# Feed-forward products over both parts of the activations at once, with the two halves of PSUM joined in later turns

## The chip, the cores and the metric

The kernel runs on one core of one Trainium2 chip. The metric is the device time of one execution in microseconds (us); the time before is 1494.89 us, the median of three runs (1494.23 to 1496.46). The engines are PE (TensorE: matrix products, written to PSUM), PEld (its weight loads), DVE (VectorE), ACT (ScalarE) and POOL (GpSimd). SP issues the DMAs.

## The reference

Three transformer blocks over 256 tokens of width 1024, in fp32, batch 1. The first has sliding-window and differential attention, cross attention and a feed-forward part with a squared ReLU. The second and the third are wrapped in SwiGLU feed-forward parts and modulated by a vector c, with a convolution and latent-attention mixer in the one and a sparse attention in the other:

```python
u = rms_norm(x, g_mlp[l]) @ w_up[l]                 # 1024 -> 4096
x = x + jnp.square(jax.nn.relu(u)) @ w_down[l]      # 4096 -> 1024
...
mod = c_act @ ada_w[l] + ada_b[l]                   # 1024 -> 9 x 1024, per layer l
h = modulate(x, norm_g[l, 0], sh1, sc1)
x = x + 0.5 * g1[:, None] * swiglu(h, ff_w13[l, 0], ff_w2[l, 0])   # 1024 -> 2 x 2816 -> 1024
...
def swiglu(h, w13, w2):
    a, b = jnp.split(h @ w13, 2, axis=-1)
    return (jax.nn.silu(a) * b) @ w2
```

SwiGLU runs four times (layer 0 and 1, before and after the mixer). The weights are some 300 MB, each read once.

## The kernel before

**Layout.** Activations lie transposed: channels on the 128 partitions, the 256 tokens (S) along the free axis. A weight tile of 128 x 128 is the stationary side of a product, a chunk of activations of 128 channels the moving one.

**Two parts.** For accuracy every operand is split into a high part (rounded to the fast fp32r format) and a low part (the rest). A product of weights w and activations x is three on PE, high by high, high by low and low by high: `mm3` (L358), 256 columns each. ACT makes the high part of the weights (`whi`), DVE the low one (`wlo`, L415), 1024 columns at a time, which is a group of eight tiles. `hhi` and `hlo` are the parts of a stage's input, `gh` and `gl` those of a feed-forward part's inner activations.

**The stream.** All weights come by DMA through four raw buffers of 1 MB (`raw`, RAW_BUFS = 4), each two groups; `issue` (L386) sends a DMA when a buffer is free, which for weights is after the second group's `wlo`. `pump` (L402) splits three groups ahead of PE; the `wlo` of a group is issued one group behind its `whi`. `run` (L435) takes the steps in a list one after another; each engine works off its own instructions in the order in which they were issued. Work put into `deferred` is issued by `flush` (L430) at the next group.

**The ten feed-forward stages.** `pairs` (L462) runs w_up (16 pairs) and the four w13 (22 pairs each): a pair is two output blocks of 128 channels, 16 tiles, two groups. The first pairs after a norm (the head: three in w13_00, two in each other w13, none in w_up) run on the input before normalisation and keep a form of their own. At the end of a pair an evacuation takes the two blocks out of one PSUM bank: `evac_up` (L1353, ReLU with the norm's factor on DVE, square on ACT) or `evac` in `ff` (L1403, SiLU on ACT, product on DVE, both from PSUM). The split into `gh` and `gl` waits in `deferred`. `singles` (L516) runs w_down (8 output blocks of 32 tiles) and the four w2 (8 blocks of 22); its evacuation `residual` (L1265) adds a block to x and begins the next norm.

**The modulation.** 72 further buffers of 1 MB (`ada`) pass through the same four raw buffers, between the weights, from 97 us on to the first third of w2_10. A piece is scaled in place by ACT and added by POOL (`adacc`, L737); the buffer is free after POOL's last addition. Its sums pass PE into a PSUM bank with the tag "T".

**Pools.** Activations that live long lie in 64 buffers of 256 columns (`g`, GP = 64). PSUM has eight banks: two each with the tags mm, T, S and O.

Of the kernel before, what the change touches and what calls it, by code (L numbers as in the profile page):

```python
# [24 lines left out]
P = 128  # L25
S = 256
# [15 lines left out]
GP = 64  # L42
# [250 lines left out]
class Kernel:  # L293
    def __init__(self, tc, ctx, dram, out):
# [63 lines left out]
    def mm3(self, out, w, x, start, stop, swap=False):  # L358

        (wh, wl), (xh, xl) = w, x  # L360
        prod = [(wh, xh), (wh, xl), (wl, xh)]
        if swap:
            prod = [(xh, wh), (xh, wl), (xl, wh)]
        for n, (l, r) in enumerate(prod):
            self.mm(out, l, r, start=start and n == 0, stop=stop and n == 2)

# [95 lines left out]
    def pairs(self, name, x, kc, evac, unit0=0, npairs=None, st=None, head=0, tags=("mm", "mm"),  # L462
              biased=None):
# [25 lines left out]
        for s0 in range(0, total, sub_tiles):  # L489
            def fn(hi, lo, s0=s0):  # L490
                for t in range(s0, min(s0 + sub_tiles, total)):
# [1345 lines left out]
```

## Time and profile before

| | us |
|---|---|
| median of the runs | 1494.89 |
| the profiled execution | 1491.65 |
| its span, first to last instruction | 1489.9 |
| PE, DVE, ACT, POOL busy in the span | 1437.3, 1059.5, 918.9, 633.6 |
| w_up, w_down (us from the span's start) | 243 to 340, 343 to 441 |
| w13_00, w2_00 | 441 to 577, 577 to 642 |
| w13_01, w2_01 | 756 to 886, 887 to 954 |
| w13_10, w2_10 | 954 to 1085, 1085 to 1150 |
| w13_11, w2_11 | 1288 to 1416, 1417 to 1480 |

The two digits of a w13 or w2 are the layer and the first or second feed-forward part in it. The ten windows make 980 us, two thirds of the span. The granted PE clock is 1.00 of full speed in every one of them (0.995 over the span). A share of busy time is an average over its window; the chain of waits is followed back from the end of the window, at each step to what released it.

### The profile page before, as it was taken

How to read it: one execution, taken by the hardware profiler on the slowest of the kernel's cores; microseconds unless marked ns; L12 is line 12 of the kernel's file. 1: busy time of each engine (PE TensorE's matmuls, PEld its weight loads, DVE VectorE, ACT ScalarE, POOL GpSimd, SP SyncE). 2: the span in 40 equal slices, each digit the busy share in tenths (PEclk: the TensorE clock that was granted, in tenths of full speed). 3: DMA queues.
4: the chain of work that ended last, by engine and by line, in shares of the span. 5: the costliest groups of instructions: out<-in, count | busy, mean ns of one | idle time of the engine just before them, and what ended most of it. 6: DMA issues, size and time to landing. Idle time of an engine off the chain costs nothing.

```text
span 1489.9 us, 28338 instructions
## 1 busy us (share of the span) xinstructions
PE 1437.3 (96%) x11478; PEld 1374.9 (92%) x11478; DVE 1059.5 (71%) x1643; ACT 918.9 (62%) x1666; POOL 633.6 (43%) x466
## 2 busy tenths in 40 slices
PE   8998999999999999998899999999999999999997
PEld 8886989999989989998799999999999887999997
DVE  7877767776658777689887776677765788765553
ACT  6546767777657567664667666676654665644442
POOL 3002433545874566753356658546453200500021
PEclk9999999999999999999999999999999999999998
DMA  8344646777665777754447877568773620355451
GB/s 319 116 142 170 218 151 227 244 270 273 260 246 199 278 267 272 257 186 170 169 171 272 295 262 296 206 238 300 259 278 132 219 80 25 118 198 196 173 182 45
DMA packets 46067, 312.00 MB, mean 209 GB/s; under 512 B 5232, under 2 KB 7024, under 8 KB 9072
## 3 DMA queue, kind: packets, MB, share of 16 engines
q1 hardware_dynamic: 45936, 310.19, 57.8%
q8 instruction: 90, 1.47, 0.4%
q14 instruction: 41, 0.34, 0.1%
HBM read 309.12 MB, written 1.05 MB: 208 GB/s over the span
## 4 chain that ended last, share of the span: by engine, by line
PE 64%; DVE 16%; ACT 8%; DMA 7%; issue 2%; POOL 1%; SPq 0%; POOLq 0%; ACTq 0%; DVEq 0%
PE mm L356 57%; DVE wlo L415 6%; DMA raw<-w 4%; ACT whi L329 2%; ACT raw L329 2%; PE sc L356 2%; PE o L356 1%; DVE p L849 1%; POOL adacc L737 1%; PE mmt L356 1%; DVE hlo L664 1%; DMA raw<-w_up 1%; DMA raw<-w_down 1%; DVE gl L353 1%; ACT p L329 1%
## 5 line engine op out<-in xcount | busy, mean ns | idle before, releaser
L415 DVE TENSOR_TENSOR wlo<-raw,whi 128x1024 fp32r<-128x1024 f32 (+2 forms) x438 | 627.2, 1438 | 52.2 <-ACT whi L329 51.7
L737 POOL TENSOR_TENSOR adacc<-adacc,raw 128x512 f32<-128x512 f32 x252 | 430.8, 1734 | 415.8 <-ACT raw L329 331.4
L356 PE MATMUL mm<-hlo,whi 128*128 128x256 f32 x1960 | 556.6, 284 | 6.0 <-DVE hlo L664 4.1
L356 PE MATMUL mm<-hhi,whi 128*128 128x256 f32 (+1 forms) x1960 | 558.0, 285 | 1.5 <-ACT whi L329 1.5
L356 PE MATMUL mm<-hhi,wlo 128*128 128x256 f32 (+1 forms) x1960 | 553.3, 282 | 5.2 <-DVE wlo L415 5.2
L329 ACT ACTIVATE whi<-raw 128x1024 fp32r<-128x1024 f32 (+2 forms) x438 | 453.2, 1044 | 110.6 <-DMA raw<-w 72.5
L356 PEld LDWEIGHTS mm<-hlo,whi 128*128 128x128 f32 x1960 | 369.9, 189 | 9.6 <-DVE hlo L664 5.6
L356 PEld LDWEIGHTS mm<-hhi,wlo 128*128 128x128 f32 x1960 | 371.2, 189 | 7.3 <-DVE wlo L415 7.0
L356 PEld LDWEIGHTS mm<-hhi,whi 128*128 128x128 f32 x1960 | 370.2, 189 | 5.4 <-DVE wlo L415 1.7
L356 PE MATMUL mm<-gh,whi 128*128 128x256 f32 x960 | 272.6, 284 | 0.0
L356 PE MATMUL mm<-gh,wlo 128*128 128x256 f32 x960 | 271.6, 283 | 0.0
L356 PE MATMUL mm<-gl,whi 128*128 128x256 f32 x960 | 271.6, 283 | 0.0
L356 PEld LDWEIGHTS mm<-gh,whi 128*128 128x128 f32 x960 | 184.2, 192 | 4.3 <-issue 3.4
L356 PEld LDWEIGHTS mm<-gl,whi 128*128 128x128 f32 x960 | 184.2, 192 | 0.0
L356 PEld LDWEIGHTS mm<-gh,wlo 128*128 128x128 f32 x960 | 184.2, 192 | 0.0
L329 ACT ACTIVATE raw<-raw,sc 128x512 f32<-128x512 f32 x252 | 167.0, 712 | 0.6 <-DMA raw<-ada 0.5
L1410 DVE TENSOR_TENSOR ft<-mm,ft 128x256 f32<-128x256 f32 x79 | 33.4, 423 | 110.0 <-ACT ft L329 109.8
L353 DVE TENSOR_TENSOR gl<-ft,gh 128x256 fp32r<-128x256 f32 x120 | 74.0, 628 | 46.2 <-ACT gh L329 46.0
L580 POOL TENSOR_SCALAR xg<-x,M 128x256 f32<-128x256 f32 x40 | 55.9, 1398 | 97.4 <-DVE x L1273 91.2
L329 ACT ACTIVATE p<-sc,nm 128x128 f32<-128x128 f32 (+1 forms) x120 | 49.8, 420 | 66.5 <-DVE r L840 18.7
L329 ACT ACTIVATE ft<-mm 128x256 f32<-128x256 f32 x79 | 29.9, 379 | 96.3 <-PE mm L356 96.1
L596 POOL TENSOR_TENSOR acc<-acc,sq 128x256 f32<-128x256 f32 x60 | 60.8, 1016 | 43.5 <-ACT sq L329 37.0
(298 smaller groups left out, 1878.6 us busy)
## 6 DMA issues: line engine op xcount, KB each, us to landing
raw<-w SPq DMA_DIRECT2D x132, 1024.0 KB, 4.9
raw<-ada SPq DMA_DIRECT2D x72, 1024.0 KB, 6.4
raw<-w_up SPq DMA_DIRECT2D x16, 1024.0 KB, 5.0
raw<-w_down SPq DMA_DIRECT2D x16, 1024.0 KB, 5.2
raw<-hy_in SPq DMA_DIRECT2D x8, 1024.0 KB, 5.2
raw<-w_in SPq DMA_DIRECT2D x6, 1024.0 KB, 7.8
raw<-nsa_in SPq DMA_DIRECT2D x6, 1024.0 KB, 5.0
raw<-w_ck SPq DMA_DIRECT2D x4, 1024.0 KB, 4.9
```

Of the source, the lines that this page charges most:

```text
L329: return self.nc.scalar.activation(out, in_, func, **k)
L353: self.nc.vector.tensor_tensor(lo, src, hi.bitcast(F), OP.subtract)
L356: self.nc.tensor.matmul(out, lhsT, rhs, start=start, stop=stop, skip_group_check=True)
L415: self.behind = lambda hi=hi[:, :b - a], lo=lo[:, :b - a], src=src: self.nc.vector.tensor_tensor(lo, src, hi.bitcast(F), OP.subtract)
L580: nc.gpsimd.tensor_scalar(st["xg", c], xc, gain(c), None, op0=OP.mult)
L596: nc.gpsimd.tensor_tensor(acc, st["acc" + key], sq, OP.add)
L664: nc.vector.scalar_tensor_tensor(*last, op0=OP.add, op1=OP.subtract)
L737: nc.gpsimd.tensor_tensor(half, half, src, OP.add)
L849: nc.vector.tensor_scalar(p[n], p[n], r[:, n:n + 1], None, op0=OP.mult)
L1410: nc.vector.tensor_mul(s, ps[:, 1, :], s)
```

## The change

In the ten stages the three products of a tile become two: `mm2` multiplies the weights' high part with both parts of the activations, which lie side by side, in one product of 512 columns over a whole PSUM bank, and adds the low part by the high activations to one half of that bank. Each block of a wide pair has a bank of its own, so two halves must be summed. `summed` copies one half of each block out with ACT and adds the other with DVE, at the end of the pair; what was the evacuation (`up`) is issued at the next group, and the split into parts one group later. In `singles` each half is added to x in an operation of its own. All other products keep the three of 256 columns (`mm3w`, `mm3`). The activations' buffers become 32 of 512 columns, which hold both parts of one tensor or two tensors of 256 columns; the sums of the modulation move from the PSUM tag T to O.

```diff
-GP = 64
+GP = 32
+PAIRED = {"un", "posi", "mem", "kz", "ra", "tab", "qr", "qd", "kd", "vd", "ck", "cv", "cq", "xpT", "od", "q", "k", "v",
+          "kb", "xg", "vcz", "p0", "cu"}
...
     def g(self, name, dt=F, shape=None):
-        return self.gp.tile(shape or [P, S], dt, name=name, tag="g")
+
+        key = (name if name in PAIRED else "", dt)
+        t = self.half.pop(key, None)
+        n = 1
+        if t is None:
+            n = 0
+            t = self.half[key] = self.gp.tile([P, 2, S], dt, name=name, tag="g")
+        ap = t[:, n, :]
...
+    def two(self, name):
+
+        if name == "gg":
+            self.half.clear()
+        t = self.gp.tile([P, 2, S], R, name=name, tag="g")
+        return t[:, 0, :], t[:, 1, :], t.rearrange("p a b -> p (a b)")
...
+    def summed(self, pss):
+
+        ts = [self.t("ft") for _ in pss]
+        for t, ps in zip(ts, pss):
+            self.act(t, ps[:, 0, :])
+        for t, ps in zip(ts, pss):
+            self.nc.vector.tensor_add(t, ps[:, 1, :], t)
+        return ts
...
+    def mm2(self, out, w, x, start, stop):
+
+        (wh, wl), (xh, _, both) = w, x[:3]
+        self.mm(out.rearrange("p a b -> p (a b)"), wh, both, start=start, stop=False)
+        self.mm(out[:, self.hi_at(x), :], wl, xh, start=False, stop=stop)
...
     def flush(self):
-        for f in self.deferred:
+
+        now, self.deferred = self.deferred, []
+        for f in now:
             f()
-        self.deferred.clear()
...
-                        if r == 0:
+                        if r == 0 and wide:
+                            state["ps"] = [self.ps("mm", [P, 2, S], "mm"), self.ps("mm", [P, 2, S], "T")]
+                        elif r == 0:
                             state["ps"] = self.ps("mm", [P, 2, S], tags[pr % 2])
-                        self.mm3(state["ps"][:, m, :], w, (xh, xl), start=r == 0, stop=k == kc - 1)
+                        if wide:
+                            self.mm2(state["ps"][m], w, x(k), start=k == 0, stop=k == kc - 1)
+                        else:
+                            self.mm3w(state["ps"][:, m, :], w, (xh, xl), start=r == 0, stop=k == kc - 1)
...
-                            state[m] = self.ps("mm", [P, S], "S" if early else "mm")
+                            state[m] = self.ps("mm", [P, S], "S") if early else self.ps("mm", [P, 2, S], "mm")
...
+                    if early:
+                        self.mm3w(state[m], w, x(k)[:2], start=first, stop=k == kc - 1)
+                    else:
+                        self.mm2(state[m], w, x(k), start=first, stop=k == kc - 1)
...
+    def h_part(self, c):
+
+        return self.h[:, c, S:2 * S], self.h[:, c, :S], self.h[:, c, :2 * S], None
...
-                ps = self.ps("ada", [P, 512], "T")
+                ps = self.ps("ada", [P, 512], "O")
...
-                if gate is None:
-                    nc.vector.tensor_add(xc, ps, xc)
-                else:
-                    nc.vector.scalar_tensor_tensor(xc, ps, gate(m), xc, op0=OP.mult, op1=OP.add)
+                for part in (ps,) if len(ps.shape) == 2 else (ps[:, 0, :], ps[:, 1, :]):
+                    if gate is None:
+                        nc.vector.tensor_add(xc, part, xc)
+                    else:
+                        nc.vector.scalar_tensor_tensor(xc, part, gate(m), xc, op0=OP.mult, op1=OP.add)
...
-            for m in range(2):
-                t = self.t("ft")
-                nc.vector.scalar_tensor_tensor(t, ps[:, m, :], 0.0, stu["rbs"], op0=OP.max, op1=OP.mult)
-                self.act(t, t, AF.Square)
-                gh, gl = self.g("gh", R), self.g("gl", R)
-                self.deferred.append(lambda gh=gh, gl=gl, t=t: self.split(gh, gl, t))
-                gg[2 * pr + m] = (gh, gl)
...
+            for m, t in enumerate(self.summed(ps)):
+                g = gg[2 * pr + m] = self.two("gg")
+
+                def up(g=g, t=t):
+                    nc.vector.scalar_tensor_tensor(t, t, 0.0, stu["rbs"], op0=OP.max, op1=OP.mult)
+                    self.act(t, t, AF.Square)
+                    self.deferred.append(lambda: self.split(g[0], g[1], t))
+                self.deferred.append(up)
...
-            else:
-                self.act(s, ps[:, 0, :], AF.Silu)
-                nc.vector.tensor_mul(s, ps[:, 1, :], s)
-            gh, gl = self.g("gh", R), self.g("gl", R)
-            self.deferred.append(lambda: self.split(gh, gl, s))
-            gg[pr] = (gh, gl)
+                self.deferred.append(lambda: self.split(g[0], g[1], s))
+                return
+            s, t = self.summed(ps)
+
+            def up():
+                self.act(s, s, AF.Silu)
+                nc.vector.tensor_mul(s, t, s)
+                self.deferred.append(lambda: self.split(g[0], g[1], s))
+            self.deferred.append(up)
```

PE in w13_11. Before, two tiles, the last of one group of weights (`whi_17261`) and the first of the next; one bank `mm_17368` takes both blocks of the pair:

```order
L356 MATMUL mm_17368<-hhi_15679,whi_17261 128x256
L356 MATMUL mm_17368<-hlo_15680,whi_17261 128x256
L356 MATMUL mm_17368<-hhi_15679,wlo_17262 128x256
L356 MATMUL mm_17368<-hhi_15679,whi_17294 128x256
L356 MATMUL mm_17368<-hlo_15680,whi_17294 128x256
L356 MATMUL mm_17368<-hhi_15679,wlo_17295 128x256
```

After, two tiles of one group, one for each block of the pair; each block has a bank, and `h` holds both parts:

```order
L386 MATMUL mm_15346<-h_13877,whi_15254 128x512
L386 MATMUL mm_15346<-h_13877,wlo_15255 128x256
L386 MATMUL mm_15347<-h_13877,whi_15254 128x512
L386 MATMUL mm_15347<-h_13877,wlo_15255 128x256
L386 MATMUL mm_15346<-h_13877,whi_15254 128x512
```

The product with `whi` has both parts in it, the one with `wlo` follows; the instructions of a tile go from three to two.

ACT in w13_11, one pair of groups. Before, `ft<-mm` is the SiLU out of PSUM:

```order
L329 ACTIVATE whi_16337<-raw_16097 128x1024
L329 ACTIVATE ft_16365<-mm_16312 128x256
L329 ACTIVATE whi_16370<-raw_16097 128x1024
L329 ACTIVATE gh_16368<-ft_16365 128x256
L329 ACTIVATE whi_16403<-raw_16176 128x1024
L329 ACTIVATE ft_16431<-mm_16378 128x256
```

After, two copies out of two banks stand where the SiLU stood; the SiLU is `ft<-ft`:

```order
L350 ACTIVATE gg_14781<-ft_14782 128x256
L350 ACTIVATE ft_14837<-mm_14796 128x256
L350 ACTIVATE ft_14838<-mm_14797 128x256
L350 ACTIVATE whi_14843<-raw_14627 128x1024
L350 ACTIVATE ft_14837<-ft_14837 128x256
L350 ACTIVATE whi_14869<-raw_14682 128x1024
L350 ACTIVATE gg_14836<-ft_14837 128x256
```

The split's high part (`gh`, now `gg<-ft`) has moved from behind the second `whi` of a buffer to behind the first `whi` of the next one, just ahead of the next pair's copies.

DVE in w13 stages, one pair of groups; `raw_16003` and `raw_14462` are buffers of weights. Before:

```order
L1410 TENSOR_TENSOR ft_16299<-mm_16246,ft_16299 128x256
L415 TENSOR_TENSOR wlo_16272<-raw_16003,whi_16271 128x1024
L353 TENSOR_TENSOR gl_16303<-ft_16299,gh_16302 128x256
L415 TENSOR_TENSOR wlo_16305<-raw_16003,whi_16304 128x1024
L1410 TENSOR_TENSOR ft_16365<-mm_16312,ft_16365 128x256
L415 TENSOR_TENSOR wlo_16338<-raw_16097,whi_16337 128x1024
```

After:

```order
L383 TENSOR_TENSOR gg_14616<-ft_14617,gg_14616 128x256
L378 TENSOR_TENSOR ft_14672<-mm_14631,ft_14672 128x256
L378 TENSOR_TENSOR ft_14673<-mm_14632,ft_14673 128x256
L457 TENSOR_TENSOR wlo_14650<-raw_14462,whi_14649 128x1024
L1471 TENSOR_TENSOR ft_14672<-ft_14673,ft_14672 128x256
L457 TENSOR_TENSOR wlo_14679<-raw_14462,whi_14678 128x1024
L383 TENSOR_TENSOR gg_14671<-ft_14672,gg_14671 128x256
L378 TENSOR_TENSOR ft_14727<-mm_14686,ft_14727 128x256
```

Ahead of the first `wlo` of a buffer stand two additions from PSUM, where the SiLU's product stood; the product now stands ahead of the second `wlo`, which frees the buffer, and `gg` behind it, where `gl` stood ahead of it.

## Rows read from the trace of the kernel before

**Rows 1.** The page: busy us (share of the span) xinstructions of an engine.

```profile
PE 1437.3 (96%) x11478; PEld 1374.9 (92%) x11478; DVE 1059.5 (71%) x1643; ACT 918.9 (62%) x1666; POOL 633.6 (43%) x466
```

**Rows 2.** Chain of waits by line: w_up, w_down, w13_00, w2_00, w13_01, w2_01, w13_11.

```profile
by line: PE mm L356 29.3%; DMA raw<-w_up 16.7%; ACT whi L329 12.7%; DVE wlo L415 8.4%; ACT raw L329 7.9%; ACT ft L329 5.4%; DVE gl L353 5.3%; issue 3.5%; ACT gh L329 3.2%; POOL adacc L737 2.7%; PE ada L356 2.0%; DVE ft L1356 1.6%; PE ssum L
by line: PE mm L356 59.3%; DMA raw<-w_down 15.4%; DVE wlo L415 7.4%; POOL adacc L737 4.6%; issue 4.4%; ACT raw L329 2.7%; PE ada L356 1.5%; ACT whi L329 1.2%; DVE hlo L574 0.9%; PE adat L760 0.9%; ACT sq L329 0.8%; DVE x L1271 0.5%; DVE hhi
by line: DMA raw<-w 22.9%; PE mm L356 22.0%; DVE wlo L415 13.0%; ACT whi L329 8.4%; POOL adacc L737 6.0%; ACT raw L329 5.2%; DVE gl L353 3.7%; PE mmt L356 3.2%; ACT ft L329 2.5%; issue 2.4%; DVE hlo L664 1.7%; DVE ft L1407 1.3%; PE ssum L35
by line: PE mm L356 98.1%; PE ada L356 1.6%; PE adat L760 0.6%
by line: PE mm L356 88.3%; DVE hlo L664 2.3%; PE mmt L356 2.2%; DVE wlo L415 2.2%; PE ada L356 0.8%; DVE gl L353 0.7%; DVE hlo L666 0.7%; PE ssum L356 0.6%; DVE ft L1407 0.6%; ACT ft L329 0.4%; PE rb L356 0.4%; PE adat L760 0.3%; DVE un L48
by line: DMA raw<-w 31.8%; PE mm L356 24.1%; DVE wlo L415 12.3%; issue 5.4%; POOL adacc L737 5.2%; ACT whi L329 4.8%; ACT raw L329 4.0%; ACT L334 1.9%; ACT adacc L329 1.8%; ACT hhi L329 1.6%; PE ada L356 1.6%; ACT sq L329 1.5%; DVE x L1273 
by line: PE mm L356 89.1%; DVE hlo L664 2.4%; PE mmt L356 2.2%; DVE wlo L415 2.2%; DVE gl L353 0.7%; DVE hlo L666 0.7%; PE ssum L356 0.6%; DVE ft L1407 0.6%; ACT ft L329 0.4%; PE rb L356 0.4%; DVE un L480 0.3%; ACT rbs L329 0.3%; issue 0.1%
```

**Rows 3.** Windows in w_up, w13_00, w13_01, w13_11: busy us (xcount) of PE, PEld, DVE, ACT, POOL.

```profile
262.00:340.00 78.00, 75.88 (x633) 75.35 (x632) 57.01 (x76) 59.68 (x108) 40.59 (x27) 1.00 0.76 266
460.00:545.00 85.00, 83.20 (x686) 81.97 (x685) 69.09 (x78) 57.85 (x94) 47.71 (x27) 1.00 0.69 250
780.00:850.00 70.00, 70.00 (x589) 70.00 (x588) 51.20 (x51) 49.86 (x78) 45.95 (x26) 1.00 0.80 286
1310.00:1410.00 100.00, 100.00 (x839) 100.00 (x839) 54.49 (x72) 46.25 (x72) 0.00 (x0) 1.00 0.55 191
```

**Rows 4.** Timeline of PE, products of 512 columns: start us, duration us, engine, operation.

```profile
67.74 0.39 PE L356 MATMUL mm<-wlo,hhi 128*128 128x512 f32 x1
...
70.07 0.39 PE L356 MATMUL mm<-whi,hlo 128*128 128x512 f32 x1
...
113.33 0.40 PE L356 MATMUL mm<-wlo,hmh 128*128 128x512 f32 x1
...
115.61 0.39 PE L356 MATMUL mm<-whi,hml 128*128 128x512 f32 x1
```

**Rows 5.** Groups by line: busy us, mean ns of one, then idle time before.

```profile
L1410 DVE TENSOR_TENSOR ft<-mm,ft 128x256 f32<-128x256 f32 x79 | 33.4, 423 | 110.0 <-ACT ft L329 109.8
L329 ACT ACTIVATE ft<-mm 128x256 f32<-128x256 f32 x79 | 29.9, 379 | 96.3 <-PE mm L356 96.1
L353 DVE TENSOR_TENSOR gl<-ft,gh 128x256 fp32r<-128x256 f32 x120 | 74.0, 628 | 46.2 <-ACT gh L329 46.0
L1273 DVE SCALAR_TENSOR_TENSOR x<-mm,M,x 128x256 f32<-128x256 f32 x48 | 23.1, 481 | 67.5 <-PE mm L356 67.4
```

**Rows 6.** Timeline of DVE in w13_01, then of POOL in the same stretch.

```profile
802.53 2.31 DVE L415 TENSOR_TENSOR wlo<-raw,whi 128x1024 fp32r<-128x1024 f32 x1
805.36 0.42 DVE L1410 TENSOR_TENSOR ft<-mm,ft 128x256 f32<-128x256 f32 x1 [0.51 <-ACT ft L329]
...
808.43 1.21 DVE L415 TENSOR_TENSOR wlo<-raw,whi 128x1024 fp32r<-128x1024 f32 x1
...
802.29 5.93 POOL L737 TENSOR_TENSOR adacc<-adacc,raw 128x512 f32<-128x512 f32 x3
```

**Rows 7.** Waits of ACT in w_up, w13_00, w13_01 (two rows), w13_11: us, times, longest.

```profile
ACT ft L329 <- DVE ft L1356: 11.0, 7, 1.9
ACT whi L329 <- DMA raw<-w_up: 7.3, 4, 3.3
...
ACT whi L329 <- DMA raw<-w: 22.2, 7, 5.3
...
ACT whi L329 <- DMA raw<-w: 10.0, 6, 3.2
ACT ft L329 <- PE mm L356: 8.0, 9, 1.8
...
ACT ft L329 <- PE mm L356: 51.5, 17, 3.2
```

More of the change, by code (lines that the diff above doesn't have):

```diff
@@ L303, in __init__ @@
         self.flip, self.now = 0, None
+        self.half = {}
         self.deferred, self.behind = [], None
     def g(self, name, dt=F, shape=None):
-        return self.gp.tile(shape or [P, S], dt, name=name, tag="g")
+        key = (name if name in PAIRED else "", dt)
[5 more added lines that the diff above has]
+        ap = t[:, n, :]
+        if shape:
+            names = " ".join(f"d{i}" for i in range(len(shape) - 1))
+            ap = ap.rearrange(f"p ({names}) -> p {names}", **{f"d{i}": x for i, x in enumerate(shape[1:])})
+        return ap
+    def two(self, name):
[3 more added lines that the diff above has]
+        return t[:, 0, :], t[:, 1, :], t.rearrange("p a b -> p (a b)")
     def w(self, name, shape, dt=F, tag=None, bufs=2):
@@ L356, in mm, with mm3, mm3w, hi_at @@
         self.nc.tensor.matmul(out, lhsT, rhs, start=start, stop=stop, skip_group_check=True)
-    def mm3(self, out, w, x, start, stop, swap=False):
+    def mm3(self, out, w, x, start, stop):
         (wh, wl), (xh, xl) = w, x
[L361 to L364, printed above, removed]
+        for n, (l, r) in enumerate([(xh, wh), (xh, wl), (xl, wh)]):
             self.mm(out, l, r, start=start and n == 0, stop=stop and n == 2)
+    def mm3w(self, out, w, x, start, stop):
+        (wh, wl), (xh, xl) = w, x
+        for n, (l, r) in enumerate([(wh, xh), (wh, xl), (wl, xh)]):
+            self.mm(out, l, r, start=start and n == 0, stop=stop and n == 2)
+    def mm2(self, out, w, x, start, stop):
+        (wh, wl), (xh, _, both) = w, x[:3]
+        self.mm(out.rearrange("p a b -> p (a b)"), wh, both, start=start, stop=False)
+        self.mm(out[:, self.hi_at(x), :], wl, xh, start=False, stop=stop)
+    def hi_at(self, x):
+        return 1 if len(x) > 3 else 0
     def stream_init(self, steps):
@@ L462, in pairs @@
     def pairs(self, name, x, kc, evac, unit0=0, npairs=None, st=None, head=0, tags=("mm", "mm"),
-              biased=None):
+              biased=None, wide=False):
         steps, state = [], {}
@@ L899, in split_out @@
     def split_out(self, ps, name, scale=None):
-        hi, lo = self.g(name + "h", R), self.g(name + "l", R)
+        pair = self.two(name)
+        hi, lo = pair[:2]
         if scale is None:
@@ L905, in split_out @@
             self.nc.vector.scalar_tensor_tensor(lo, ps, scale, hi.bitcast(F), op0=OP.mult, op1=OP.subtract)
-        return hi, lo
+        return pair
     def zeroed(self, name, keep):
@@ L965, in late_loads @@
         nc.sync.dma_start(self.posi[1], self.dram["pos"][:, 1, :])
-        self.mem = [self.g(f"mem{c}") for c in range(KD)]
+        self.mem = [self.g("mem") for c in range(KD)]
         for c in range(KD):
@@ L1067, in mdst @@
         def mdst(c):
-            hm[c] = (self.g(f"hmh{c}", R), self.g(f"hml{c}", R))
+            hm[c] = self.two("hm")
             return hm[c]
@@ L1460, in evac_z @@
                         nc.vector.tensor_mul(a, src, a)
-                        hi, lo = self.g("yh", R), self.g("yl", R)
-                        self.split(hi, lo, a)
-                        y[c] = (hi, lo)
+                        y[c] = self.two("y")
+                        self.split(y[c][0], y[c][1], a)
         scale = 96 ** -0.5
@@ L1474, in qdst @@
         def qdst(c):
[L1475 removed]
+            cqn[c] = self.two("cqn")
             return cqn[c]
         def kdst(c):
[L1479 removed]
+            ckvn[c] = self.two("ckvn")
             return ckvn[c]
```

58 lines of the change are left out of this document (27 added, 31 removed).

## The prediction

> **What bounds the kernel now.** I read the page's engine totals first, then the chain of waits cut by stage, then busy times in steady stretches, then what ScalarE (ACT) waits for. The reader is to see a kernel that TensorE (PE) seems to fill, and in part doesn't. PE is busy 1437.3 of 1489.9 us [rows 1]. But the chain that sets the end lies on PE's products only in some of the ten feed-forward stages [rows 2]: 98.1% of w2_00, 88.3% of w13_01, 89.1% of w13_11 and, with rows like these, w13_10, w2_10 and w2_11. In w_up it is 29.3%, in w13_00 22.0%, in w2_01 24.1%, in w_down 59.3%; there it goes round a loop: a raw weight buffer lands, ACT makes its high part, VectorE (DVE) its low part, the buffer is free, the next DMA goes out. The steady stretches say the same [rows 3]: in w13_11 (no modulation weights, POOL idle) DVE is busy 54% and ACT 46% of the time, in w13_01 73% and 71%, in w_up 73% and 77%, in w13_00 81% and 68%. And ACT has nothing left in w_up: 59.68 us busy and 11.0 + 7.3 us of waits for DVE and DMA make up the 78 us [rows 3, 7], so it never waits for PE there. In w13_00 it waits 22.2 us for DMA, in w13_01 10.0 for DMA and 8.0 for PE, in w13_11 51.5 for PE alone [rows 7].
>
> **The change part by part.** First the products. A tile (128 x 128 weights) takes three products of 256 columns now, and one of 512 and one of 256 after: the same 768 columns, one instruction and one weight load fewer. In w13_11 PE starts 839 products in 100 us [rows 3], one per 119.2 ns. Products of 512 columns run already where weights are the moving side: ten follow each other in 2.33 us and ten in 2.28 us [rows 4], 233 and 228 ns. Two of 256 take 238.4, so a tile saves 5.4 to 10.4 ns; I take the middle, 7.9 ns. The tiles: 16 pairs of w_up and 19 + 3 x 20 pairs of w13 beyond the heads, 16 tiles each, make 256 + 304 + 960; w_down has 256 and each w2 176; 2480 in all. In the six stages whose chain is PE (1488 tiles) the saving is 11.8 us. In the other four I count the chain's share on PE: 256 x 0.293 + 256 x 0.593 + 304 x 0.22 + 176 x 0.241 = 336 tiles, 2.7 us. Sum: 14.5 us saved, of a possible 2480 x 7.9 = 19.6.
>
> The Trainium skill ("TensorE: Matmul & The Clock Gate", section "Back-to-back issue gap") gives a spacing of N/2.4 + 2.5 ns, by which two of 256 columns and one of 512 differ by 2.5 ns only. By that the saving on these 1824 tiles would be an estimated 4.6 us; the rows show 119.2 ns where the page has 109.2, so here each product carries more than the page says, and the rows decide.
>
> Second, joining the halves. Each wide pair gets two ACT copies out of PSUM (379 ns each) and two DVE additions with one side in PSUM (423 ns as the product `ft<-mm,ft`) [rows 5]. The ReLU or the SiLU and its product then work from SBUF. Per pair that is 0.76 us of ACT and 0.85 us of DVE more, beside PE's 48 products (5.72 us before, 5.6 after). In w13_01 DVE's 51.20 us over 12.2 pairs [rows 3] are 4.19 per pair, ACT's 49.86 are 4.08. The product that now reads two SBUF tiles is priced by `gl<-ft,gh`, 628 ns [rows 5], 0.2 more. After: DVE 5.24, ACT 4.84 of 5.6. Both still fit, so I hide them behind PE in w13_01 and w13_10, and more easily in w13_11; if this cover goes, the stage takes DVE's time.
>
> Why could it go? DVE and POOL exclude each other on some operations: from 802.29 us on POOL runs three `adacc` for 5.93 us; a `wlo` that starts beside them takes 2.31 us, one that starts behind them 1.21, and an `ft` product out of PSUM in their midst keeps its 0.42 [rows 6]. The Trainium skill ("SBUF — State Buffer", section "Who interferes with whom") says that a DVE instruction with two SBUF inputs contends with POOL's reads and that one with a single SBUF input does not. This trace agrees (2.31 against 1.21, and 0.42 unmoved). By it the additions are free of POOL and the moved product is not; without it DVE would need 5.04 per pair in w13_01.
>
> In w_up and w13_00 the additions lie on the buffer loop: on DVE they stand ahead of the `wlo` that frees the buffer. In exchange `gl` moves behind that `wlo`, and the product moves between the two `wlo`. Per pair on the loop: 0.85 + 0.63 - 0.42 - 0.63 = 0.43 us. The chain is off PE for 0.71 x 16 + 0.78 x 19 = 26 pairs, so up to 11.2 us; nothing is the other end, since ACT waits for DMA there anyway, and below nothing it could gain the 11.0 us that ACT waits for DVE's `ft` in w_up [rows 7]. I take 5 us: a buffer's freeing is on the chain about every second pair (there are four).
>
> Third, the edge of a stage. Each output block of w_down and w2 is now added to x in two operations; the last one of a stage has the next norm behind it. One more of 481 ns [rows 5], five times: 2.4 us. The other 35 blocks lie beside products.
>
> At nothing: the activations laid side by side (same bytes, same writers); the buffers handed out in pairs (the same 64 halves; the cover is that the long-lived ones sit together, and if a half keeps its partner, one DVE or ACT write waits for a product, some 0.3 us at a time); the modulation rows in the "O" banks (in these stages only the norm's sum uses them); the later split of the activations (the next stage reads the last of them in its third step). PE waits for whole banks, two per row of a pair, which are free after copies and additions, 1.6 us into a pair of 5.6.
>
> Sum: -14.5 + 5 + 2.4 = -7.1 us. The profiled execution, 1491.65 us, is 3.2 under the runs' median of 1494.89; the sum is taken from the former (1484.6) and shifted by that: 1487.8, so 1488.
>
> **The rivals.** R1, PE decides everywhere: faster join work and shorter products let the early stages catch up too. For it: PE is busy 75.88 of 78 us even in w_up [rows 3]. Against it: rows 2. Time: all 2480 tiles, 19.6 - 2.4 = 17.2 less, 1478; with 10.4 ns per tile, 1471.
>
> R2, slower: ACT and DVE become the bound of the two early stages. In w_up ACT's two copies fit in no wait for PE, because there is none: 16 x 0.76 = 12.2 us. In w13_00 the 0.43 us on the loop is paid by each of 19 pairs: 8.2. With 11.8 saved in the PE stages and 2.4 at the edges: +11, 1506. It decides from the point where ACT's busy time and its waits in w_up pass 5.7 us a pair; they stand there now. Against it: waits for DMA shrink when ACT comes later, and ACT's waits for DVE's `ft` may move.
>
> R3, nothing: a product of 512 columns among others of 256 costs what two cost, for instance because the weight load behind it is no longer hidden. For it: the 512s of rows 4 stand among themselves only. Against it: both lie under 238.4. Time: 2.4 us of edges and no gain, 1497, within the bound. The page's rule on spacing named above would lie close to it, with those 4.6 us as a gain.
>
> **How the numbers follow.** Forecast 40% (own range 1481 to 1494), R1 20%, R2 23%, R3 17%. A measurement of this kernel can tell about 0.2%, 3 us, from no change. Faster by more: 0.35 of the forecast's 0.40, all of R1, 0.03 of R3: 0.58. Within: 0.05 of the forecast, 0.10 of R3, 0.01 of R2: 0.16. Slower: 0.26. The range reaches into R1 with half its mass and to R2's value: 1473 to 1506.
>
> **What would show it.** Right: starts of a 512 and the 256 behind it together about 351 ns where three took 358; w13_11 and w2_11 shorter by 2.5 and 1.4 us; w13_01 and w13_10 still on PE in the chain, with DVE above 90% busy; w_up and w13_00 not shorter. Wrong: a `mm` on PE that waits for `wlo` throughout w13_01 (then DVE bounds it and R2 spreads), ACT waiting for PE in w_up (R1), or a 512 at 238 ns or more (R3). A PE that waits for a PSUM bank, or a long wait outside the feed-forward stages, would break what I put at nothing.

## The result: 1.6% slower

The kernel with 512-column products takes 1519.49 us (median of 4 runs, 1515.93 to 1521.71), the kernel before 1495.2 (4 runs, 1494.23 to 1496.46): ratio 1.016, 95% interval 1.0138 to 1.0181. The forecast was 1488, faster. The profiled execution spans 1519.9 us, 30.0 more than the one of before; it is the slowest of its four, while the one of before (1491.65 us) lies below all four of its runs, so the profiles differ by more than the medians' 24.3 us. The page's engine totals, which answer to [rows 1]:

```profile
PE 1439.6 (95%) x8998; PEld 1249.8 (82%) x8998; DVE 1172.8 (77%) x1873; ACT 974.4 (64%) x1856; POOL 627.5 (41%) x466
```

PE is as busy as before with 2480 products fewer; DVE has 113 us more, ACT 55. Which stage pays is read from the starts of each stage's first product (us to the next stage's first product; the last one to the end of the span). The four right-hand columns are kernels of the experiments below. Every column is one execution: where a stage's code is that of before, eight profiles put w_up at 98.7 to 100.5 us, w13_00 at 135.4 to 138.1 and w13_10 at 130.2 to 131.1.

| stage | before | after | sums in PSUM | before, no additions | after, no additions | late stages wide |
|---|---|---|---|---|---|---|
| w_up | 100.2 | 111.9 | 103.8 | 95.7 | 93.9 | 100.3 |
| w_down | 97.4 | 97.3 | 98.3 | 94.3 | 92.6 | 97.4 |
| w13_00 | 136.6 | 140.4 | 136.8 | 131.4 | 129.4 | 135.6 |
| w2_00 | 65.1 | 65.5 | 64.1 | 65.1 | 62.8 | 65.3 |
| hybrid attention | 113.6 | 119.7 | 117.2 | 107.4 | 105.6 | 114.2 |
| w13_01 | 130.5 | 136.2 | 129.7 | 130.5 | 128.4 | 130.2 |
| w2_01 | 67.7 | 69.6 | 70.7 | 65.0 | 62.8 | 67.4 |
| w13_10 | 130.6 | 134.7 | 133.9 | 130.6 | 128.4 | 130.3 |
| w2_10 | 65.5 | 66.1 | 64.2 | 65.1 | 63.6 | 64.0 |
| second attention | 137.2 | 136.9 | 137.2 | 139.0 | 137.6 | 136.7 |
| w13_11 | 128.9 | 126.8 | 126.8 | 129.0 | 126.8 | 126.8 |
| w2_11 and end | 73.4 | 71.7 | 72.2 | 73.3 | 71.8 | 71.3 |

The loss (30.0 us) is w_up 11.7, hybrid attention 6.1, w13_01 5.7, w13_10 4.1, w13_00 3.8 and w2_01 1.9, against 3.9 gained in w13_11 and w2_11, where POOL has nothing to add.

The chain of waits cut by stage, as in [rows 2]: w_up, w13_00, w13_01, w13_11 of the kernel after. It is one chain, followed back from the last instruction of the run, and a window shows the part of it that lies there.

```profile
by line: DVE ft L1413 16.6%; DVE wlo L457 15.7%; ACT whi L350 11.4%; DVE gg L383 11.4%; PE mm L386 10.8%; DVE ft L378 8.1%; ACT raw L350 7.7%; ACT ft L350 7.6%; ACT gg L350 4.1%; ACT adacc L350 2.3%; issue 1.6%; PE ada L386 0.9%; PE ssum L3
by line: DMA raw<-w 24.7%; ACT whi L350 11.1%; DVE wlo L457 9.7%; PE mm L386 9.5%; ACT ft L350 6.6%; ACT raw L350 6.3%; issue 5.7%; POOL adacc L790 5.2%; PE mmt L386 3.1%; DVE ft L1471 2.9%; DVE gg L383 2.6%; ACT adacc L350 2.4%; ACT gg L35
by line: DMA raw<-w 23.9%; PE mm L386 20.8%; ACT whi L350 11.3%; ACT raw L350 8.4%; DVE wlo L457 7.1%; ACT ft L350 6.1%; issue 4.8%; DVE ft L1471 2.7%; ACT gg L350 2.3%; DVE h L715 2.2%; PE mmt L386 2.1%; POOL adacc L790 2.1%; DVE gg L383 1
by line: PE mm L386 89.1%; DVE h L715 2.4%; PE mmt L386 2.3%; DVE wlo L457 2.2%; DVE h L717 0.7%; DVE gg L383 0.7%; PE ssum L386 0.6%; DVE ft L1464 0.6%; ACT ft L350 0.4%; PE rb L386 0.4%; DVE un L523 0.3%; ACT rbs L350 0.3%; issue 0.1%; DV
```

w13_01, 88.3% on PE in [rows 2], is now at 20.8%, and goes round the buffer loop like w13_00. In w_up the largest item is one that was 1.6%: `ft L1413`, the ReLU product that the change moved from PSUM to SBUF. The steady stretches, as in [rows 3] (w_up, w13_00, w13_01, w13_11):

```profile
262.00:350.00 88.00, 78.81 (x419) 65.11 (x418) 70.76 (x97) 65.44 (x131) 40.21 (x26) 0.98 0.64 233
470.00:560.00 90.00, 84.42 (x472) 71.32 (x471) 79.48 (x102) 64.89 (x120) 45.70 (x27) 1.00 0.66 243
800.00:875.00 75.00, 72.37 (x402) 61.41 (x402) 62.99 (x76) 56.94 (x105) 40.82 (x24) 1.00 0.69 255
1340.00:1440.00 100.00, 100.00 (x571) 87.58 (x570) 69.38 (x115) 59.96 (x111) 0.00 (x0) 1.00 0.56 199
```

PE no longer fills w_up (78.81 of 88 us) or w13_01 (72.37 of 75, full before), yet DVE is only 80% and 84% busy: no single engine is full. In w13_11 PE is full, and POOL stands at 0. The products themselves cost what was expected, as two of them in w13_11 show (timeline of PE: start, duration):

```profile
1360.51 0.40 PE L386 MATMUL mm<-h,whi 128*128 128x512 f32 x1
1360.74 0.29 PE L386 MATMUL mm<-h,wlo 128*128 128x256 f32 x1
1360.87 0.40 PE L386 MATMUL mm<-h,whi 128*128 128x512 f32 x1
```

A 512 starts, the 256 follows after 0.23 us and the next 512 0.13 behind that, 0.36 here; over the whole of w13_11 the medians are 232 and 118 ns, and 351 from one 512 to the next, from the starts in the trace.

The groups that answer to [rows 5] (busy, mean ns of one, idle time before), over the whole run:

```profile
L378 DVE TENSOR_TENSOR ft<-mm,ft 128x256 f32<-128x256 f32 x190 | 71.6, 416 | 42.8 <-ACT ft L350 42.8
L383 DVE TENSOR_TENSOR gg<-ft,gg 128x256 fp32r<-128x256 f32 x120 | 68.1, 579 | 45.9 <-ACT gg L350 45.7
L1471 DVE TENSOR_TENSOR ft<-ft 128x256 f32<-128x256 f32 x79 | 65.6, 830 | 14.5 <-ACT ft L350 14.5
L1413 DVE SCALAR_TENSOR_TENSOR ft<-ft,rbs 128x256 f32<-128x256 f32 x32 | 25.1, 825 | 0.0
```

The same view of w13_01 and then of w13_11, DVE:

```profile
L1471 DVE TENSOR_TENSOR ft<-ft 128x256 f32<-128x256 f32 x12 | 9.4, 784 | 4.7 <-ACT ft L350 4.7
...
L1471 DVE TENSOR_TENSOR ft<-ft 128x256 f32<-128x256 f32 x18 | 7.5, 418 | 0.0
```

The added sums, with one side in PSUM, take 416 ns. The moved products, which now read two SBUF tiles (`ft<-ft` names the same pool twice), take 830 and 825; I had priced them at 628. In w13_01 it is 784, in w13_11, without POOL, 418. These means mix two prices. Of the 32 products of w_up the shortest, the median and the longest (ns) are:

```profile
L1413 DVE SCALAR_TENSOR_TENSOR ft<-ft,rbs x32: 410/418/1516, 253.0 to 359.4; 128x256 f32<-128x256 f32 x32
```

In the trace, the 12 that overlap an `adacc` of POOL take 1507 ns on average, the 20 with POOL idle 416 at the median. What holds them up is seen in w_up, in the timelines of DVE and of POOL over one stretch, as in [rows 6]:

```profile
264.09 0.74 DVE L378 TENSOR_TENSOR ft<-mm,ft 128x256 f32<-128x256 f32 x2
264.75 1.21 DVE L457 TENSOR_TENSOR wlo<-raw,whi 128x1024 fp32r<-128x1024 f32 x1
265.88 2.94 DVE L1413 SCALAR_TENSOR_TENSOR ft<-ft,rbs 128x256 f32<-128x256 f32 x2
268.75 1.21 DVE L457 TENSOR_TENSOR wlo<-raw,whi 128x1024 fp32r<-128x1024 f32 x1
273.04 0.75 DVE L1413 SCALAR_TENSOR_TENSOR ft<-ft,rbs 128x256 f32<-128x256 f32 x2
```

```profile
264.91 3.64 POOL L790 TENSOR_TENSOR adacc<-adacc,raw 128x512 f32<-128x512 f32 x2 [20.41 <-ACT raw L350]
```

While POOL runs its two additions (3.64 us), the two moved products need 2.94 us; with POOL idle, at 273.04, they need 0.75. The sums out of PSUM keep 0.74.

### The profile page after: what moved, and what is told of

Read it like the earlier page. It is cut to its first block, busy times and chain, and to the rows that moved or that the text cites. A ratio compares the mean times of both kernels' runs of the same rounds, so it can differ in the third digit from the quotient of the medians.

```text
span 1519.9 us, 23822 instructions
## 1 busy us (share of the span) xinstructions
PE 1439.6 (95%) x8998; PEld 1249.8 (82%) x8998; DVE 1172.8 (77%) x1873; ACT 974.4 (64%) x1856; POOL 627.5 (41%) x466
## 4 chain that ended last, share of the span: by engine, by line
PE 46%; DVE 22%; ACT 14%; DMA 10%; issue 4%; POOL 3%; SPq 0%; POOLq 0%; ACTq 0%; DVEq 0%
PE mm L386 39%; DVE wlo L457 8%; DMA raw<-w 8%; ACT whi L350 5%; ACT raw L350 3%; POOL adacc L790 3%; ACT ft L350 2%; PE sc L386 2%; DVE gg L383 2%; PE o L386 2%; DVE h L715 1%; PE mmt L386 1%; DVE ft L1413 1%; DVE p L902 1%; DVE ft L1471 1%
## 5 line engine op out<-in xcount | busy, mean ns | idle before, releaser
L386 PE MATMUL mm<-h,whi 128*128 128x512 f32 (+2 forms) x2400 | 714.5, 359 | 7.1 <-DVE h L715 4.4
L386 PE MATMUL mm<-h,wlo 128*128 128x256 f32 (+1 forms) x1960 | 559.4, 285 | 22.9 <-DVE wlo L457 22.0
L350 ACT ACTIVATE whi<-raw 128x1024 fp32r<-128x1024 f32 (+2 forms) x438 | 453.6, 1045 | 98.0 <-DMA raw<-w 71.3
L386 PEld LDWEIGHTS mm<-h,whi 128*128 128x128 f32 x2400 | 427.7, 191 | 80.4 <-DVE h L715 8.2
L386 PEld LDWEIGHTS mm<-h,wlo 128*128 128x128 f32 x1960 | 372.5, 190 | 38.5 <-DVE wlo L457 37.9
L386 PE MATMUL mm<-gg,whi 128*128 128x512 f32 x960 | 335.8, 394 | 2.6 <-DVE gg L383 2.4
L386 PE MATMUL mm<-gg,wlo 128*128 128x256 f32 x960 | 268.1, 279 | 1.3 <-DVE wlo L457 1.3
L386 PEld LDWEIGHTS mm<-gg,whi 128*128 128x128 f32 x960 | 179.8, 187 | 48.0 <-DVE gg L383 3.5
L386 PEld LDWEIGHTS mm<-gg,wlo 128*128 128x128 f32 x960 | 181.0, 189 | 2.2 <-DVE wlo L457 2.2
L378 DVE TENSOR_TENSOR ft<-mm,ft 128x256 f32<-128x256 f32 x190 | 71.6, 416 | 42.8 <-ACT ft L350 42.8
L386 PE MATMUL mm<-o,whi 128*128 128x256 f32 x448 | 83.5, 287 | 1.3 <-DVE x L1326 1.2
L1471 DVE TENSOR_TENSOR ft<-ft 128x256 f32<-128x256 f32 x79 | 65.6, 830 | 14.5 <-ACT ft L350 14.5
L386 PEld LDWEIGHTS mm<-o,whi 128*128 128x128 f32 x448 | 70.2, 191 | 3.7 <-DVE x L1326 1.6
```

The source lines that it names most:

```text
L350: return self.nc.scalar.activation(out, in_, func, **k)
L378: self.nc.vector.tensor_add(t, ps[:, 1, :], t)
L386: self.nc.tensor.matmul(out, lhsT, rhs, start=start, stop=stop, skip_group_check=True)
L1471: nc.vector.tensor_mul(s, t, s)
```

## The experiments

Theory T1: the join tips the stages that carry the modulation off PE, and mainly by the moved products, which are held up beside POOL's additions. Rivals: T2, the new layout (paired buffers, h side by side, another PSUM bank) costs; T3, the single-tile stages' extra addition costs; and, inside T1, plain load: 0.76 us of ACT and 0.85 of DVE per pair are too much whatever POOL does. "Before" is run beside every kernel on the same chip. The diffs are shortened, with the kernels' switches written out as their values.

**The layout alone.** The paired stages and the single-tile stages get their three products of 256 and their old evacuations back (w_up's is not shown):

```diff
-            s, t = self.summed(ps)
+            s = self.t("ft")
+            self.act(s, ps[:, 0, :], AF.Silu)
+            nc.vector.tensor_mul(s, ps[:, 1, :], s)
...
-                        self.mm2(state[m], w, x(k), start=k == 0, stop=k == kc - 1)
+                        self.mm3w(state[m], w, x(k)[:2], start=first, stop=k == kc - 1)
```

> Every product is again three of 256 columns and every evacuation is the one of before; what stays of the change is its layout: buffers in pairs, hi and lo of h side by side, the modulation's PSUM tile in the bank tagged O. Theory T1 (the joining work on ScalarE and VectorE slows the stages that also carry the modulation): the layout costs nothing, 1495 us, within 3 of before, and the hybrid stage has its 114 us again. Rival T2 (the layout itself costs, as the hybrid stage's 113.6 to 119.7 us suggests): 1501 us or more, with the hybrid stage at 118 to 120.

1494.1 us, before 1493.73: ratio 1.0006 (0.9996 to 1.0016), hybrid attention 114.1 us. T2 falls: the layout costs nothing, and the hybrid's 6 us are not its doing.

**Single tiles wide, pairs narrow.** The first half of that diff alone, in all pairs.

> The 512-column product in the single-tile stages alone (w_down and the four w2), where no joined pair arises but one extra VectorE add per tile; pairs stay narrow. T1: the w2 stages without a pair's join are on TensorE, so they gain what the spacing gives, 1.4 us each at most, and nothing else loses: 1489 to 1493 us. Rival T3 (the singles' extra add and longer PSUM turn are what costs, as w2_01's 67.6 to 69.5 us suggests): above 1496.

1494.46, ratio 1.0011 (0.9999 to 1.0023): above the 1489 to 1493 expected, so T1's gain is missed, and below the 1496 that T3 needs. In its profile w2_00, w2_10 and w2_11 (to its last product) are 1.1, 1.0 and 2.3 us shorter, but w2_01 is 3.2 longer and the hybrid attention 5.5. Where w2_01's went is in the section on the hardware.

**The sum stays in PSUM.** A sum that afterwards meets another SBUF operand is written back over its PSUM half, so that the moved product reads one side from PSUM again. Same instructions, same count:

```diff
-            self.nc.vector.tensor_add(t, ps[:, 1, :], t)
+            self.nc.vector.tensor_add(ps[:, 1, :] if n in keep else t, ps[:, 1, :], t)
...
-                nc.vector.tensor_mul(s, t, s)
+                nc.vector.tensor_mul(s, u, s)     # u = ps[1][:, 1, :]
```

> The changed kernel, but a joined sum that afterwards meets another SBUF operand is left in PSUM, so that no VectorE product of the join reads two SBUF tiles: same count of instructions on every engine. If the join hurts by the moved product's 830 ns, that is, by VectorE and GpSimd waiting for each other on SBUF (T1 with the port): the product falls to about 0.45 us, w_up, w13_01 and w13_10 win back 3 to 5 us each, 1505 us or below. If it hurts by plain load of VectorE and ScalarE and by PSUM held longer (T1 without the port): 1515 to 1522.

1500.49, before 1493.73: ratio 1.0059 (1.0036 to 1.0082). The excess over before falls from 24.3 to 6.8 us, by the place of the sum alone. The moved products in its profile (DVE groups of the whole run; then those of w_up):

```profile
L1472 DVE TENSOR_TENSOR ft<-mm,ft 128x256 f32<-128x256 f32 x79 | 32.9, 417 | 19.1 <-ACT ft L350 19.1
```

```profile
L457 DVE TENSOR_TENSOR wlo<-raw,whi 128x1024 fp32r<-128x1024 f32 x25 | 37.0, 1480 | 0.0
L383 DVE TENSOR_TENSOR gg<-ft,gg 128x256 fp32r<-128x256 f32 x26 | 16.7, 684 | 14.9 <-ACT gg L350 14.9
L1413 DVE SCALAR_TENSOR_TENSOR ft<-mm,rbs 128x256 f32<-128x256 f32 x24 | 8.9, 411 | 0.0
```

417 and 411 ns instead of 830 and 825, and w_up, w13_00 and w13_01 win back 8.1, 3.6 and 6.5 us (table); w13_10, of which 3 to 5 were expected, wins only 0.8. What still reads two SBUF tiles (`wlo`, `gg`) still pays beside POOL: 1480 and 684 ns here. And the sum in PSUM has a price of its own. What PE waits for in w_up (us in total, times, longest), after and then here:

```profile
PE mm L386 <- DVE wlo L457: 7.4, 9, 1.7
```

```profile
PE mm L386 <- DVE ft L1413: 6.7, 5, 1.7
```

The waits for `wlo` are gone, but PE now waits for the moved product, which must read its sum before PE can have the bank again.

**A stage without modulation.** Singles wide, and of the pairs only w13_11; in the others:

```diff
-                        biased=evac, wide=True)
+                        biased=evac, wide=(l, f) == (1, 1))
```

> The 512-column product in all single-tile stages and, of the paired stages, only in w13_11, the one without modulation work. T1: as the kernel with wide singles alone, less w13_11's 2.1 us: 1487 to 1491 us, faster than both kernels. T2 and T3: no better than 1496.

1492.58, ratio 0.9991 (0.998 to 1.0002): 1.9 us better than the singles alone, as w13_11 says (126.8 us instead of 128.6), but not the 1487 to 1491 that I expected, because the singles had not paid.

**POOL's additions left out.** Before, and after, each without the line that adds a piece to the running sum:

```diff
-                    nc.gpsimd.tensor_tensor(half, half, src, OP.add)
```

> The kernel before without GpSimd's additions of the modulation (each sum keeps its first piece only, so the modulation is incomplete; ScalarE's scaling and all DMAs stay). It is the base for the next kernel and not a candidate. Expected by T1: the weights' low parts fall from 1.44 to about 1.22 us; 1475 to 1492 us, since before most stages are on TensorE anyway.

> The changed kernel without GpSimd's additions of the modulation (the same part left out). T1, the lock (the join costs because the product of two SBUF tiles and GpSimd's additions hold each other up): the product takes 0.42 us throughout, and the change is now a gain over the base without additions: 6 to 15 us less than it. Rival, plain load (the join's 1.6 us per pair on VectorE and ScalarE is too much whatever GpSimd does): 5 us or more above that base.

Before falls to 1462.61 (ratio 0.9801, 0.9785 to 0.9817), more than the 1475 to 1492 expected; after falls to 1442.5 (0.9662, 0.9646 to 0.9679). Without POOL's additions the same change is worth 20.1 us (6 to 15 were expected), where beside them it costs 24.3. Plain load whatever POOL does falls: the join is complete in this kernel. The chains in w_up, before and after without additions, then the DVE groups of w13_01 after:

```profile
by line: PE mm L356 97.4%; PE ada L356 1.1%; PE ssum L356 0.8%; PE rb L356 0.5%; PE adat L759 0.5%
by line: PE mm L386 97.2%; PE ada L386 1.1%; PE ssum L386 0.8%; PE rb L386 0.5%; PE adat L812 0.5%
```

```profile
L457 DVE TENSOR_TENSOR wlo<-raw,whi 128x1024 fp32r<-128x1024 f32 x39 | 47.4, 1217 | 0.0
L378 DVE TENSOR_TENSOR ft<-mm,ft 128x256 f32<-128x256 f32 x38 | 14.5, 421 | 7.4 <-ACT ft L350 7.4
L383 DVE TENSOR_TENSOR gg<-ft,gg 128x256 fp32r<-128x256 f32 x19 | 8.0, 423 | 13.6 <-ACT gg L350 13.6
L1470 DVE TENSOR_TENSOR ft<-ft 128x256 f32<-128x256 f32 x18 | 7.6, 423 | 9.9 <-ACT ft L350 9.9
```

w_up, 29.3% on PE in [rows 2], is at 97.4% in the kernel before without additions, so the loop through ACT, DVE and the buffers was itself a consequence of them. This pair of kernels doesn't tell two ways apart: without additions no product waits for one, and the modulation's raw buffers come free earlier; it is the sum in PSUM that points to the product. The moved product takes 423 ns, `gg` 423, `wlo` 1217. Against its base all ten feed-forward stages gain (table).

**The join without the 512.** Banks, sums and evacuations of the change, but each 512 as two of 256:

```diff
-        self.mm(out.rearrange("p a b -> p (a b)"), wh, both, start=start, stop=False)
+        self.mm(out[:, n, :], wh, xh, start=start, stop=False)
+        self.mm(out[:, 1 - n, :], wh, xl, start=False, stop=False)
```

> The changed kernel with its banks, its join and its evacuations, but each 512-column product as two of 256. T1: where the join bounds the stage the time is as in the changed kernel, and only the stages on TensorE (w13_11, w2_11, w2_10, part of w2_00) lose their 7 to 11 ns per tile, 1523 to 1532 us. Rival (the 512-column product itself is the trouble, by longer bursts and gaps or the clock): 1512 us or less.

1523.51, ratio 1.0212 (1.0193 to 1.0231): as T1 has it. The join alone costs 30.6 us, and the 512 gives back 4.0 of it by the two medians, 6.3 with each against its own before. The rival, trouble in the 512 itself, falls as the main cause. A part of it stays: in the profiles the hybrid attention takes 114.3 us here and w13_01 133.4, against 119.7 and 136.2 with the 512.

**Only late stages wide.** w2_10, w13_11 and w2_11, everything else narrow:

```diff
-                    if early:
+                    if early or name not in ("w2_10", "w2_11"):
```

> The 512-column product in w2_10, w13_11 and w2_11 alone, the stages where the earlier runs show a gain with no loss behind it (0.9, 2.1 and 2.3 us): 1488.5 us, ratio 0.9965, with the granted clock of the earlier stages as before. If the gains are given back at the next wait on GpSimd's sums, or at the end, 1493 to 1495.

1488.63 against 1492.92: ratio 0.9966 (0.9952 to 0.9979), as expected. This beats both kernels. (The table's column is an execution of 1484.28 us.)

**One stage more.** The same with w2_00, with w2_01, and with w13_01 (its second sum left in PSUM) wide as well.

> As the kernel with w2_10, w13_11 and w2_11 wide, and w2_00 wide too. T1 with the clock: w2_00 is 1.0 us shorter, but TensorE reaches the hybrid stage's first weights ahead of them and its gaps there are followed by more stretches at a granted clock of 0.5: the hybrid stage takes 1 to 4 us more, in all 1488 to 1492 us. Rival (the gain of a stage on TensorE stays): 1487.6 us, hybrid stage 114 us.

> As the kernel with w2_10, w13_11 and w2_11 wide, and w2_01 wide too. T1 with the wait: TensorE meets the modulation's row sums earlier, waits there for GpSimd's additions some 3 us instead of 1.2, and the granted clock then falls to 0.5 for some 6 us: w2_01 takes 70 to 71 us instead of 67.4, 1490.5 to 1492.5 us in all. Rival (the wide product is paid as in w2_11): w2_01 at 65 to 66 us, 1486.5 us.

> As the kernel with w2_10, w13_11 and w2_11 wide, and w13_01 wide too, its second sum left in PSUM, so that no product of the join reads two SBUF tiles. From the run in which all stages were so: w13_01 at 129.7 us instead of 130.2, 1488 us in all, no difference that can be measured from the kernel without it; the full rate of TensorE (128.3 us, as without GpSimd's additions) would give 1486.7. Plain load theory: above 1490.

1489.79 (0.9978, 0.9968 to 0.9988), 1488.04 (0.997, 0.996 to 0.9979) and 1492.2 (0.9995, 0.9983 to 1.0007), beside before at 1492.72. The first lies in its range, but its profile has the hybrid only 0.7 us longer than the kernel it builds on, with less half clock rather than more (1.7 us lost there against 5.1), so the reason given is not shown. The second has w2_01 at 70.4 us with the wait and the half clock expected, and yet runs as fast as without it: a miss by 2.5 us; the profile is of one execution of 1490.58 us, so its loss in w2_01 isn't shown to be that of the median. The third is a miss too: w13_01 takes 132.7 us, not 129.7, and its chain is off PE again. The time is what plain load was to give (above 1490), beside POOL's additions:

```profile
by line: DMA raw<-w 28.3%; PE mm L389 21.8%; ACT whi L353 12.1%; ACT raw L353 7.7%; DVE wlo L460 6.1%; ACT ft L353 5.6%; issue 3.1%; DVE h L718 2.3%; PE mmt L389 2.1%; ACT gg L353 2.1%; POOL adacc L793 2.1%; DVE ft L1489 0.9%; DVE gg L386 0
```

Its profile also has 2.3 us more in the hybrid attention and 2.9 in w2_01 than the kernel that it builds on, stages with the same code in both. Leaving the sum in PSUM doesn't make w13_01 pay beside POOL's additions. No further wide stage is shown to gain.

## Why the prediction was wrong, by its own steps

*The products* were priced rightly: 351 ns for a 512 and a 256 (expected about 351), w13_11 2.1 us shorter (expected 2.5), w2_11 2.3 from its first product to its last (expected 1.4). But of the 14.5 us in the sum only these two stages' gain came. Without POOL's additions all ten stages pay, and the difference of 20.1 us is R1's case (17.2). The Trainium skill ("TensorE: Matmul & The Clock Gate", section "Back-to-back issue gap") gives N/2.4 + 2.5 ns, which the prediction took as the spacing of products in a stream, for an isolated product. In the stream of w13_11 the starts lie 232 and 118 ns apart. Which stages PE decides was read from the chain of before, and that was the weak point: the change itself moved w13_01 and w13_10 off PE.

*The join* is the step that failed: "Both still fit, so I hide them behind PE in w13_01 and w13_10". Instead of -2.5 us each they cost +5.7 and +4.1. The sum put the moved product at 628 ns, a mean over stages with POOL idle and busy; one takes 0.42 us without POOL's additions and some 1.5 beside one, which makes 784 ns on average in w13_01 and 825 in w_up. [Rows 6] had shown the mutual exclusion, and I used it to acquit the additions and then let the product, the one instruction of the join that moves into it, pay only 0.2 us. DVE's busy time also was the wrong measure: at 84% it did not bound w13_01 by itself (it was to pass 90%). A DVE that is late frees the raw buffer late, the next DMA starts late, and the chain shows `DMA raw<-w` at 23.9%. "A `mm` that waits for `wlo` throughout w13_01" came, if not throughout. PE's waits over the whole run, first one of before, then two of after, then those in 800 to 875 us, w13_01:

```profile
PE mm L356 <- DVE wlo L415: 5.2, 8, 1.9
...
PE mm L386 <- DVE wlo L457: 23.3, 37, 1.7
PE ada L386 <- POOL adacc L790: 9.8, 10, 1.7
...
PE mm L386 <- DVE wlo L457: 2.6, 5, 0.6
```

The waits for `wlo` grew from 5.2 to 23.3 us, those for `adacc` from 3.8 to 9.8; in the steady part of w13_01, the last row is all of PE's 2.6 idle us.

The Trainium skill ("SBUF — State Buffer", section "Who interferes with whom") calls the port pair that DVE and POOL share an exclusive lock. The runs agree, with sizes: the product takes 417 ns with one side in PSUM and 422 with both in SBUF and POOL not adding, but some 1.5 us with both in SBUF beside an addition.

*The loop of w_up and w13_00*, +5 of a possible 11.2, came to 11.7 + 3.8. "A buffer's freeing is on the chain about every second pair" fell: 16.6% of the 108 us of w_up's window, 17.9, are moved products on the chain, of 25.1 in all. R2's figure for w_up (12.2) is near by luck, from another cause: it blamed ACT's copies, and with all of these kept the sum in PSUM takes w_up's loss from 11.7 to 3.6 us. R2 also kept the gains of the PE stages, which is why it stopped at 1506.

*The edges*, +0.48 each: the stretch from the last product of w2_11 on grew from 10.2 to 10.8 us, near the price. Over the profiles of all kernels the stretch behind that product's end is 9.5 to 9.9 us without the second addition and 10.0 to 11.0 with it; the other edges can't be told apart.

*At nothing*: the layout held (1494.1 against 1493.73). PE did wait for a bank, which was to be nothing: in w_up 1.5 us for the additions that free it (`ft L378`). What I did not look for is the hybrid attention's 6.1 us, next section. R3 fell (351 ns).

Still open is a part of the rest of the sum-in-PSUM kernel, 6.8 us above before, where without POOL's additions the change is worth 20.1: w_up (+3.6), w13_10 (+3.3), hybrid attention and w2_01 (+3.6, +3.0). In w_up PE waits for the bank (6.7 us above), in w13_10 1.1 us for the same reason. In the hybrid attention and w2_01 3.4 us of clock each are lost beyond before. What `wlo` and `gg` beside POOL add to this no run separates, and the same code for w13_01 took 129.7 us in one kernel and 132.7 in another.

## What to carry to other kernels

Before moving a VectorE operand from PSUM to SBUF, look which engine shares SBUF with VectorE at that moment, and price the instruction by rows beside that engine, not by a mean over the run. Leaving the operand in PSUM avoids that wait, but holds the bank longer. A stage "on PE" in the chain is so by a margin: what its suppliers gain in work must be tested against the loop of buffers and DMAs, not against their busy share. Make such a change stage by stage: here three of ten stages pay for it, and all ten together cost more than five times what these gain.

## What the hardware showed beside this

TensorE's granted clock fell to 0.50 (1.2 of 2.4 GHz) behind gaps of some microseconds. Windows of w2_01, first of the kernel with all singles wide, then of before: PE, PEld, DVE, ACT, POOL busy, then PEclk.

```profile
940.00:944.00 4.00, 4.00 (x22) 2.59 (x20) 3.37 (x4) 3.94 (x6) 4.00 (x3) 1.00 0.98 412
944.00:947.00 3.00, 0.83 (x4) 0.14 (x2) 1.83 (x1) 2.08 (x3) 3.00 (x4) 1.00 1.02 429
947.00:954.00 7.00, 5.84 (x14) 3.40 (x14) 3.40 (x4) 2.62 (x6) 2.31 (x3) 0.53 0.71 246
954.00:961.00 7.00, 7.00 (x43) 6.17 (x42) 2.07 (x7) 0.74 (x1) 0.68 (x1) 0.98 0.18 73
```

```profile
935.00:943.00 8.00, 8.00 (x61) 6.56 (x59) 6.00 (x6) 6.61 (x9) 8.00 (x6) 1.00 0.95 368
943.00:945.00 2.00, 0.84 (x3) 0.14 (x2) 2.00 (x2) 0.00 (x0) 1.17 (x1) 1.00 0.27 111
945.00:955.00 10.00, 10.00 (x83) 9.81 (x83) 3.23 (x10) 3.25 (x6) 1.66 (x2) 1.00 0.55 211
```

What PE waited for in the middle of it, first in the one with singles wide, then before (us in total, times, longest):

```profile
PE ada L389 <- POOL adacc L793: 3.3, 2, 2.2
```

```profile
PE ada L356 <- POOL adacc L737: 1.2, 1, 1.2
```

Before, PE met the modulation's row sums and waited 1.2 us for POOL's additions; it kept its clock. With shorter products it came there earlier and waited 3.3 us; it then ran at a granted 0.53 for the next 7 us, and where w2_00 and w2_10 gained 1 us the stage lost 3.2. Two things keep this from being the whole cause. In the join without the 512 and in the kernel with w13_01 wide, w2_01 has its three products of 256, and PE waits there for POOL's additions 2.3 and 2.7 us, twice each; the stage takes 69.3 and 70.3 us at a full clock. And the length of the wait doesn't decide alone what the clock does. The same place after, and then with w2_01 wide in the kernel with late stages wide:

```profile
PE ada L386 <- POOL adacc L790: 2.8, 2, 1.7
```

```profile
PE ada L389 <- POOL adacc L793: 2.8, 2, 1.7
```

The waits are alike; after, the clock stays at 1.00 (965 to 984 us), and in the other kernel it is 0.51 over the next 7 us. In the hybrid attention, first after, then before:

```profile
700.00:709.00 9.00, 9.00 (x73) 8.80 (x72) 8.32 (x14) 6.46 (x11) 3.24 (x3) 1.00 0.59 225
709.00:714.00 5.00, 0.12 (x1) 0.00 (x0) 4.83 (x13) 1.40 (x3) 0.00 (x0) 0.78 0.63 228
712.00:718.00 6.00, 3.44 (x14) 3.38 (x15) 5.83 (x13) 1.06 (x1) 0.00 (x0) 0.50 0.36 126
```

```profile
688.60:693.80 5.20, 0.00 (x0) 0.00 (x0) 5.04 (x12) 2.38 (x3) 0.00 (x0) 1.00 0.60 208
693.80:697.40 3.60, 3.38 (x14) 3.31 (x15) 3.49 (x7) 0.00 (x0) 0.00 (x0) 0.53 0.46 148
```

After, PE does 0.12 us of work in 5 us, the clock falls, and 6 us run at 0.50. Before, the same gap is there (5.4 us in both, for DVE's `q`), and the clock is at half for 3.4 us. Lost clock, as the sum of (1 - granted) over 10-us windows of the hybrid stage, is 10.2 us after (stage 119.7), 1.7 before (113.6), 3.4 with the layout alone (114.1), 1.7 in the join without 512 (114.3) and 8.6 with all singles wide (119.1), but 5.1 in the kernel with late stages wide, at 114.2. PE's idle time in the stage hardly differs, 12.3 us before and 12.7 after (between products, in the trace), so most of the hybrid's 6 us are products at half clock and not wider gaps. The mean granted clock of all runs, not only the profiled ones, goes with the 512 beside POOL's additions: its median is 0.993 before on three chips, 0.9925 with the layout alone, 0.994 in the join without 512 and 0.995 after without additions, but 0.989 after and 0.990 with all singles wide. Why the clock falls more often or for longer behind the same gaps isn't settled.
